# A hybrid decoder block on one core: modulation products put off, queries and keys normed in pairs, a row of numbers in PSUM, the last expert products ordered by tiles of tokens

## The chip, the cores and the metric

One core of one Trainium2 chip. The metric is the device time of the program in microseconds; three runs of the kernel before have a median of 2023.93 us (2022.27 to 2029.1). The engines are named as the profile names them: PE (matmuls), DVE (vector), ACT (scalar), POOL (GpSimd), SP (the queue that issues nearly all DMAs).

## The reference, cut to what matters

```
mod = silu(c) @ w_ada + b_ada                      # 6 x 1024 numbers: sh1, sc1, gt1, sh2, sc2, gt2
xn  = rms_norm(h) * (1 + sc1) + sh1                # 512 tokens x 1024 channels
qm, km, vm, zrw, gate_logits = split(xn @ w_in)
qm, km = rope(rms_norm(qm, q_norm_g)), rope(rms_norm(km, k_norm_g))     # per head of 64 channels
h   = h + gt1 * ((gated attention(qm, km, vm) + gated rwkv7(zrw)) @ w_out)
xn2 = rms_norm(h) * (1 + sc2) + sh2
s   = xn2 @ wq against 2 x 128 sub-keys, 8 heads; 16 best of each half; 16 best of their sums -> idx, gates
h   = h + gt2 * sum_k gelu(xn2 . u[idx_k]) * gates_k * v[idx_k]         # 16384 experts
```

The experts are computed densely for tokens 128 to 511 (all 128 groups of 128 experts, with a dense matrix of gates), and by gathered rows for tokens 0 to 127.

## The kernel before, in words

All of float32 is kept by splitting each operand into a high and a low part (`whi`, `wlo`; `vh`, `vl`; `ah`, `al`) and adding three products. Each engine runs its instructions in a fixed order, which a scheduler has written out at build time from the program's order, its priorities and the ordering hints that `follow(i, after)` gives; no hint costs a semaphore. The parts that matter here:

**Modulation.** `mod_col(ci, j)` multiplies a row block of `w_ada` (tile `wmod`, 512 KB, three buffers) by silu(c) and sums it on DVE, one instruction of 128x1024 (L176). Sixteen are needed at the start (sh1, sc1). The other 32, for gt1, gt2, sc2 and sh2, come from a generator, and `mods(1, i)` at the end of every product of a weight block (`w_cm`, L423; `w_tm`, twice, L456) takes one of them. `gate_rows` needs gt1 and gt2 after the twelfth gate product; sc2 and sh2 are needed in `out_norm`.

**Mixing.** `rwkv_in` computes the inputs of the recurrence (`decays`, `elementwise`, by DVE, POOL and ACT), with the products of L422 on PE. The recurrence over four chunks of 128 tokens (`inverses`, `tokens`, `state`, `group_norm`, tile `rwp`, L387) has a high priority, and other products fill PE between its steps: queries, keys and values (`qkv`, `w_tm`, L452), then attention and the sixteen gate products (`gates`, L422). In `qk_part`, for each half of the tokens, ACT copies the product to SBUF and squares it, DVE sums it per head and takes 1/sqrt by three Newton steps (12 instructions on 128x8, L574 and L161 to L166), POOL applies the gain and the rotation, DVE scales (`qn`, L589), and PE transposes the result (L594).

**Experts.** `queries` scores the sub-keys into PSUM (tile `atp`, three banks, L994) and finds the best 16 on DVE. `best_of` makes 50 candidates and picks their numbers: DVE compares (`eq`, L1026, 128x400, the row of numbers `iota` in SBUF), POOL (DVE for one tile of tokens) multiplies (L1027), DVE sums (L1029). `gates_dense` builds two one-hot matrices for each four tokens (`oh2`, L1221, on DVE, from a copy of `iota` that lies in PSUM; `ohg`, L1225 on DVE or L1230 and L1231 on ACT) and multiplies them on PE (`pg`, L1238), 96 times. Amid these, `dense_h` runs the products with U (L1178), its low parts on POOL (L1172). Then `dense_v` and `products` add the products with V into six PSUM banks `acc` (token tile t in banks 2t and 2t+1, L1305); the last two groups of experts are done together. At the end DVE scales each bank (L1335), DVE or POOL adds the residual (L1336), and SP stores it.

Of the kernel before, what the change touches and what calls it, by code (L numbers as in the profile page):

```python
# [10 lines left out]
F32 = mybir.dt.float32  # L11
# [5 lines left out]
ALU = mybir.AluOpType  # L17
# [12 lines left out]
NCAND = 50  # L30
# [33 lines left out]
def kernel(ctx: ExitStack, tc: tile.TileContext, A):  # L64
# [332 lines left out]

    nsplit = [0]

    def wload(src):  # L400
# [14 lines left out]
    def w_cm(w, x, k0, nk, n=512):  # L415

        hi, lo = w
        ps = mmtile()
        for k in range(nk):
            ks = slice((k0 + k) * 128, (k0 + k + 1) * 128)  # L420
            for n, (l, r) in enumerate(((hi, x[0]), (hi, x[1]), (lo, x[0]))):
                i = fill(PE.matmul(ps, l[:, ks], r(k), start=k == 0 and n == 0, stop=k == nk - 1 and n == 2), 512)  # L422
        mods(1, i)  # L423
        return ps
# [13 lines left out]
    def w_tm(src, x, halves=False):  # L438

        pss, ws = [mmtile() for _ in range(2)], {}  # L440
        todo = [(kh, tt) for kh in range(2) for tt in range(4)]
        if halves:
            todo.sort(key=lambda t: t[1] // 2)
        for kh, tt in todo:
# [10 lines left out]
            if tt == 3:  # L455
                mods(1, i)  # L456
        return pss
# [107 lines left out]

    def qk_part(ps, hf, qi, g):
        qf = ahalf("qn")
        qn = qf.rearrange("p (h j) -> p h j", h=8)
        ACT.copy(qf, ps)
        sq = ahalf("qsq").rearrange("p (h j) -> p h j", h=8)  # L570
        ACT.activation(sq, qn, AF.Square)
        ss = sm.tile([128, 8], F32, name="qss")
        DVE.tensor_reduce(ss, sq, axis=AX.X, op=ALU.add)
        DVE.tensor_scalar(ss, ss, 1.0 / 64, 1e-6, op0=ALU.mult, op1=ALU.add)  # L574
        y = sm.tile([128, 8], F32, name="qy")
        t = sm.tile([128, 8], F32, name="qt")
        newton(ss, y, t)
        POOL.tensor_tensor(qn, qn, qkg[:, qi:qi + 1].broadcast_to([128, 8, 64]), op=ALU.mult)
        r1, r2 = [at.tile([128, 2, 4, 16], F32, name=nm, bufs=1) for nm in ("r1", "r2")]
        x = qf.rearrange("p (i h j) -> p i h j", i=2, h=4)  # L580

        def table(n, a):
            return sincos[:, 2 * hf:2 * hf + 2, n:n + 1, a:a + 8 if n else 16].broadcast_to([128, 2, 4, 8 if n else 16])

        POOL.tensor_tensor(r1, x[:, :, :, 0:16], table(0, 0), op=ALU.mult)
        for a in (0, 8):
            POOL.tensor_tensor(r2[:, :, :, a:a + 8], x[:, :, :, 8 - a:16 - a], table(1, a), op=ALU.mult)
        POOL.tensor_tensor(x[:, :, :, 0:16], r1, r2, op=ALU.add)
        DVE.tensor_tensor(qn, qn, bc3(y, 64), op=ALU.mult)  # L589
        pT = attile()  # L590
        for c in range(2):
            for i in range(2):
                o = (2 * c + i) * 128
                PE.transpose(pT[:, o:o + 128], qf[:, i * 256 + c * 128:i * 256 + (c + 1) * 128], ident)  # L594
        dst = kvhalf("qkT")
        ACT.copy(dst, pT)
        for c in range(2):
            (qT, kT)[qi][hf, 2 * g + c] = v2(dst)[:, c]

    def qkv():  # L600
        for qi in (1, 0):
            for g in range(2):
                pss = w_tm(A["w_in_t"][2 * qi + g], X)
                for hf in range(2):
                    qk_part(pss[hf], hf, qi, g)
        for tt in range(4):
            vtok[tt] = kvhalf("vtok")
        for g in range(2):
            pss = w_tm(A["w_in_t"][4 + g], X)
            for tt in range(4):  # L610
                ACT.copy(vtok[tt][:, g * 256:(g + 1) * 256], pss[tt // 2][:, (tt % 2) * 256:(tt % 2 + 1) * 256])
# [272 lines left out]
    hd_ = [dr.tile([128, 4, 2, 256], F32, name=f"h_d{i}") for i in range(2)]  # L884
    vals, inds = {}, {}

# [115 lines left out]
    def best_of(tt, hh):  # L1002
# [20 lines left out]
        for j in range(8):  # L1023
            h_, k_ = j // 2, (j % 2) * 8
            eq = qg.tile([128, 8 * NCAND], F32, name="eq", bufs=3).rearrange("p (k n) -> p k n", k=8)
            DVE.tensor_tensor(eq, bc3(bf_[:, h_, k_:k_ + 8], NCAND), bcm(iota[:, 0:NCAND], 8), op=ALU.is_equal)  # L1026
            (DVE if tt in EQD else POOL).tensor_tensor(eq, eq, ci_[:, h_:h_ + 1].broadcast_to([128, 8, NCAND]), op=ALU.mult)  # L1027
            o = (8 * hh + j) * 8
            DVE.tensor_reduce(idf[tt][:, o:o + 8], eq, axis=AX.X, op=ALU.add)  # L1029
# [53 lines left out]
    qkv()  # L1083
    attend(0)
    gates(range(G0, G1))
    attend(1)
# [159 lines left out]

    queries(out_norm(mixer(o_rwkv)))

    iop.append(attile())
    ACT.copy(iop[0][:, 0:128], iota)  # L1250
# [47 lines left out]

    def products(es, parts):
        for t in range(3):  # L1300
            ts = slice(t * 128, (t + 1) * 128)
            for e, (ah, al, vh, vl) in zip(es, parts):
                for l, r in ((ah, vh), (ah, vl), (al, vh)):
                    for d in range(2):
                        i = PE.matmul(acc[2 * t + d], l[:, ts], r[:, d * 512:(d + 1) * 512],  # L1305
                                      start=e == 0 and l is ah and r is vh, stop=e == 127 and l is al)
        return i

# [104 lines left out]
```

## Time and profile before

| | |
|---|---|
| median of three runs | 2023.93 us |
| the profiled execution | 2025.54 us, span 2023.8 us, granted TensorE clock 0.979 |
| PE busy | 1915.9 us, 95% |
| DVE busy | 1510.3 us, 75% |
| ACT, POOL busy | 828.3 us (41%), 775.6 us (38%) |
| HBM traffic over the span | 222 GB/s |

By time from the span's start: to about 100 us the start and the first products; to about 560 us the recurrence, with queries, keys, values, attention and gates between its steps; to 712 us the output projection and its norm; to 800 us the queries of the experts; to 1215 us the dense gates and the first products with U; to 2014 us the products with V and the rest of those with U; then the stores. A busy time is the union of the instructions' durations; an instruction that is held in its engine counts as busy.

### The profile page before, as it was taken

What the parts mean: (1) busy time and instruction counts of PE and PEld (TensorE: products, weight loads), DVE (VectorE), ACT (ScalarE), POOL (GpSimd) and SP (SyncE); (2) the same over time, 40 slices, a digit from 0 to 9 for tenths busy, and PEclk for the clock granted to TensorE, in tenths of its full rate; (3) what the DMA queues carried; (4) which work ended last, traced back from release to release, by engine and by line L of the source; (5) the groups of instructions that cost most, each with busy time, mean ns of one, the idle gap of its engine ahead of it and who ended that gap; (6) DMA issues with size and microseconds to landing.
All of it is one profiled execution on the core that took longest, in us unless ns stands there. A gap on an engine that the chain in (4) does not pass through costs nothing.

```text
span 2023.8 us, 29453 instructions
## 1 busy us (share of the span) xinstructions
PE 1915.9 (95%) x10509; PEld 1669.0 (82%) x10509; DVE 1510.3 (75%) x3268; ACT 828.3 (41%) x1367; POOL 775.6 (38%) x631
## 2 busy tenths in 40 slices
PE   7987899999989899888999999999999999999997
PEld 5666777787868888877899998888899999999985
DVE  7798665546445578999977876888756788888885
ACT  5443233323313433356777763333333333333332
POOL 5555210010105322566656663222212444544551
PEclk9998899999989899999999999999999999999999
DMA  8664233321446423435568989999967999999893
GB/s 288 211 202 134 81 115 98 102 93 49 156 138 195 127 80 97 131 110 165 180 199 278 322 303 388 356 354 346 333 219 245 337 335 351 326 351 331 306 346 131
DMA packets 204326, 450.79 MB, mean 223 GB/s; under 512 B 16649, under 2 KB 105225, under 8 KB 204178
## 3 DMA queue, kind: packets, MB, share of 16 engines
q1 hardware_dynamic: 167024, 314.54, 46.1%
q0 software_dynamic: 36864, 134.23, 18.3%
q8 instruction: 83, 1.36, 0.3%
q14 instruction: 65, 0.53, 0.1%
q10 hardware_dynamic: 290, 0.13, 0.0%
HBM read 393.13 MB, written 55.71 MB: 222 GB/s over the span
## 4 chain that ended last, share of the span: by engine, by line
PE 69%; DVE 17%; DMA 4%; issue 2%; ACT 1%; POOL 0%; POOLq 0%; SPq 0%; DVEq 0%; ACTq 0%
PE acc L1305 23%; PE mm L1178 17%; PE mm L422 10%; PE rwp L387 8%; PE mm L452 4%; DMA vf<-in_peer_v 2%; PE pg L1238 2%; DVE ohg L1225 2%; DVE eq L1026 2%; DVE oh L1221 1%; DVE idf L1029 1%; DVE row L1143 1%; PE atp L868 1%; PE atp L842 1%; PE atp L994 1%
## 5 line engine op out<-in xcount | busy, mean ns | idle before, releaser
L1178 PE MATMUL mm<-x,whi 128*128 128x384 f32 x2048 | 542.2, 345 | 1.7 <-ACT ge L1183 1.7
L1178 PEld LDWEIGHTS mm<-x,whi 128*128 128x128 f32 x2048 | 372.7, 190 | 5.6 <-ACT ge L1183 2.0
L1178 PE MATMUL mm<-x,wlo 128*128 128x384 f32 x1024 | 350.8, 343 | 9.5 <-POOL wlo L1172 9.5
L1171 ACT CAST whi<-wf 128x1024 fp32r<-128x1024 f32 x128 | 134.7, 1052 | 290.8 <-PE mm L1178 223.7
L1305 PE MATMUL acc<-vl,ah 128*128 128x512 f32 x768 | 237.6, 390 | 2.7 <-DVE vl L1296 2.7
L1305 PE MATMUL acc<-vh,al 128*128 128x512 f32 x768 | 237.2, 390 | 0.0
L412 POOL TENSOR_TENSOR wlo<-wf,whi 128x1024 fp32r<-128x1024 f32 x33 | 80.9, 2450 | 399.2 <-ACT whi L409 309.9
L1305 PE MATMUL acc<-vh,ah 128*128 128x512 f32 x768 | 206.7, 390 | 3.3 <-ACT vh L1295 3.2
L1178 PEld LDWEIGHTS mm<-x,wlo 128*128 128x128 f32 x1024 | 194.6, 190 | 11.1 <-POOL wlo L1172 10.9
L1172 POOL TENSOR_TENSOR wlo<-wf,whi 128x1024 fp32r<-128x1024 f32 x66 | 163.5, 2479 | 102.4 <-ACT whi L1171 102.3
L1120 POOL DMA_INDIRECT row<-in_peer_u,gidx x96 | 113.2, 1179 | 233.2 <-DVE gh L1143 223.0
L1120 POOL DMA_INDIRECT row<-in_peer_v,gidx x86 | 124.1, 1443 | 154.1 <-DVE gacc L1150 142.5
L1296 DVE TENSOR_TENSOR vl<-vf,vh 128x1024 fp32r<-128x1024 f32 x128 | 157.5, 1231 | 22.5 <-ACT vh L1295 21.9
L1305 PEld LDWEIGHTS acc<-vh,ah 128*128 128x128 f32 x768 | 143.7, 188 | 34.5 <-ACT vh L1295 5.2
L1305 PEld LDWEIGHTS acc<-vl,ah 128*128 128x128 f32 x768 | 143.6, 188 | 31.0 <-DVE vl L1296 3.5
L1305 PEld LDWEIGHTS acc<-vh,al 128*128 128x128 f32 x768 | 144.1, 188 | 30.0
L1295 ACT CAST vh<-vf 128x1024 fp32r<-128x1024 f32 x128 | 134.7, 1054 | 17.2 <-DMA vf<-in_peer_v 17.2
L422 PE MATMUL mm<-X,whi 128*128 128x512 f32 x400 | 135.7, 411 | 3.3 <-ACT z L472 3.3
L1172 DVE TENSOR_TENSOR wlo<-wf,whi 128x1024 fp32r<-128x1024 f32 x62 | 75.9, 1224 | 84.1 <-ACT whi L1171 83.9
L1238 PE MATMUL pg<-ohg,oh 128*128 128x128 f32 x768 | 117.3, 287 | 22.0 <-ACT ohg L1231 15.2
L1143 DVE CUSTOM_DVE_ANT_0 row<-row,xtok 128x1024 f32<-128x1024 f32 x96 | 131.7, 1380 | 4.4 <-DMA row<-in_peer_u,gidx 4.4
L1238 PEld LDWEIGHTS pg<-ohg,oh 128*128 128x128 f32 x768 | 108.0, 192 | 31.6 <-ACT ohg L1231 19.0
(1195 smaller groups left out, 3807.5 us busy)
## 6 DMA issues: line engine op xcount, KB each, us to landing
wf<-in_peer_ut SPq DMA_DIRECT2D x128, 512.0 KB, 4.9
vf<-in_peer_v SPq DMA_DIRECT2D x128, 512.0 KB, 6.0
wmod<-in_w_ada SPq DMA_DIRECT2D x48, 512.0 KB, 4.3
G_d<-stg SPq DMA_DIRECT2D x12, 2048.0 KB, 9.4
wf<-in_w_in_c SPq DMA_DIRECT2D x30, 512.0 KB, 3.9
ge_d<-ge SPq DMA_DIRECT2D x50, 192.0 KB, 2.5
ger<-ge_d SPq DMA_DIRECT2D x50, 192.0 KB, 6.3
wf<-in_peer_wq SPq DMA_DIRECT2D x16, 512.0 KB, 3.5
```

Of the source, the lines that this page charges most:

```text
L387: i = f(*a, **k)
L422: i = fill(PE.matmul(ps, l[:, ks], r(k), start=k == 0 and n == 0, stop=k == nk - 1 and n == 2), 512)
L452: i = fill(PE.matmul(ps[:, c0:c0 + 256], l(4 * kh + k)[:, ts], r[:, cs], start=kh == 0 and tt % 2 == 0 and k == 0 and n == 0, stop=kh == 1 ...
L1120: i = POOL.indirect_dma_start(out=row, out_offset=None, in_=A[key], in_offset=bass.IndirectOffsetOnAxis(ap=gidx[:, s_:s_ + 1], axis=0))
L1143: DVE.tensor_tensor_reduce(out=row, in0=row, in1=xtok, op0=ALU.mult, op1=ALU.add, scale=1.0, scalar=0.0, accum_out=gh[:, s_:s_ + 1])
L1171: ACT.copy(uh, f)
L1172: (POOL if e < LAG else DVE).tensor_tensor(ul, f, uh.bitcast(F32), op=ALU.subtract)
L1178: i = PE.matmul(ps[:, 0:NTD], l[:, ks], r[:, k, 128:512], start=n == 0, stop=n == 23)
L1238: i = PE.matmul(pg[:, t * 128:(t + 1) * 128], oh2[:, t], ohg[:, t], start=True, stop=True)
L1295: ACT.copy(vh, f)
L1296: DVE.tensor_tensor(vl, f, vh.bitcast(F32), op=ALU.subtract)
L1305: i = PE.matmul(acc[2 * t + d], l[:, ts], r[:, d * 512:(d + 1) * 512], start=e == 0 and l is ah and r is vh, stop=e == 127 and l is al)
```

## The change

Four edits. `mods` takes its number from `nmod`: none in the products of the recurrence's inputs and of queries and keys, one in those of the values, two in every product after the first half of attention. `qk_parts` treats both halves of a product's tokens at once: one 1/sqrt on 128x16 in place of two on 128x8, and the transposes are issued later, hinted behind the third and fourth tile of the next product. A second copy of `iota` goes into a bank of `atp` before the queries, and `eq` reads it. In the last `products`, a hint keeps the matmuls of token tile t behind those of tile t-1.

```diff
+    nmod, marks = [0], []
@@ w_cm
-        mods(1, i)
+        mods(nmod[0], i)
@@ w_tm
+        marks.clear()
...
             if tt == 3:
-                mods(1, i)
+                mods(nmod[0], i)
+            marks.append(i)
@@
-    def qk_part(ps, hf, qi, g):
-        qf = ahalf("qn")
...
+    def qk_parts(pss, qi, g):
+
+        ss, y, t = [sm.tile([128, 2, 8], F32, name=n) for n in ("qss", "qy", "qt")]
+        qfs = []
+        for hf in range(2):
+            qf = ahalf("qn")
+            ACT.copy(qf, pss[hf])
+            sq = ahalf("qsq").rearrange("p (h j) -> p h j", h=8)
+            ACT.activation(sq, qf.rearrange("p (h j) -> p h j", h=8), AF.Square)
+            DVE.tensor_reduce(ss[:, hf], sq, axis=AX.X, op=ALU.add)
+            qfs.append(qf)
         DVE.tensor_scalar(ss, ss, 1.0 / 64, 1e-6, op0=ALU.mult, op1=ALU.add)
         newton(ss, y, t)
...
+        def channels_first(after):
+            for hf, qf in enumerate(qfs):
+                pT = attile()
+                for c in range(2):
+                    for i in range(2):
+                        o = (2 * c + i) * 128
+                        m = PE.transpose(pT[:, o:o + 128], qf[:, i * 256 + c * 128:i * 256 + (c + 1) * 128], ident)
+                        follow(m, after[hf])
...
+        return channels_first
@@ qkv
                 pss = w_tm(A["w_in_t"][2 * qi + g], X)
-                for hf in range(2):
-                    qk_part(pss[hf], hf, qi, g)
+                if later:
+                    later.pop()(marks[2:4])
+                later.append(qk_parts(pss, qi, g))
...
+            nmod[0] = 1
             pss = w_tm(A["w_in_t"][4 + g], X)
+            if later:
+                later.pop()(marks[2:4])
@@ best_of
-            DVE.tensor_tensor(eq, bc3(bf_[:, h_, k_:k_ + 8], NCAND), bcm(iota[:, 0:NCAND], 8), op=ALU.is_equal)
+            DVE.tensor_tensor(eq, bc3(bf_[:, h_, k_:k_ + 8], NCAND), bcm(ioe[0][:, 0:NCAND], 8), op=ALU.is_equal)
@@
     attend(0)
+    nmod[0] = 2
@@
-    queries(out_norm(mixer(o_rwkv)))
-
+    first_q = out_norm(mixer(o_rwkv))
+
+    ioe.append(attile())
+    ACT.copy(ioe[0][:, 0:128], iota)
+    queries(first_q)
@@ products
+            ts, last = slice(t * 128, (t + 1) * 128), i
...
+                        if len(es) > 1:
+                            follow(i, last)
```

On DVE, while the recurrence's first chunk begins (`C`, `Dk`: its first inverse; `qss`, `qy`, `qt`: the 1/sqrt of the keys; `wmod`: a modulation product). Before:

```order
L166 SCALAR_TENSOR_TENSOR qy<-qt,qy 128x8
L164 TENSOR_TENSOR qt<-qy 128x8
L645 TENSOR_TENSOR Dk<-C,dl_558 128x512
L166 SCALAR_TENSOR_TENSOR qy<-qt,qy 128x8
L164 TENSOR_TENSOR qt<-qy 128x8
L165 SCALAR_TENSOR_TENSOR qt<-qt,qss 128x8
L176 ISA wmod,modc<-wmod,scr 128x1024
L176 ISA modc 128x1
L164 TENSOR_TENSOR qt<-qy 128x8
L165 SCALAR_TENSOR_TENSOR qt<-qt,qss 128x8
L166 SCALAR_TENSOR_TENSOR qy<-qt,qy 128x8
L645 TENSOR_TENSOR Dk<-C,dl_558 128x512
```

and now:

```order
L658 TENSOR_REDUCE C<-cm__1279 128x64
L166 SCALAR_TENSOR_TENSOR qy<-qt,qy 128x16
L663 TENSOR_TENSOR Dk<-C,dl_558 128x512
L595 TENSOR_TENSOR qn<-qn,qy 128x512 x2
L663 TENSOR_TENSOR Dk<-C,dl_558 128x512
L413 TENSOR_TENSOR wlo<-wf,whi 128x1024
```

The modulation product is gone from between the two `Dk`, and so are the second chains of the 1/sqrt; both scalings `qn` of a pair stand together.

On PE, the transposes of the second pair of keys (`atp<-ident,qn`) and the first matmuls that wait for the first inverse (`rwp<-ident,XT`). Before, half of the pair stood directly ahead of them:

```order
L452 MATMUL mm<-wlo,X 128x256
L594 MATMUL atp<-ident,qn 128x128 x4
L387 MATMUL rwp<-ident,XT 128x128 x4
L387 MATMUL rwp<-RR,Bq 128x128 x4
L452 MATMUL mm<-whi,X 128x256 x2
```

and now the whole pair stands amid the next product:

```order
L454 MATMUL mm<-whi,X 128x256
L603 MATMUL atp<-ident,qn 128x128 x8
L454 MATMUL mm<-whi,X 128x256
L454 MATMUL mm<-wlo,X 128x256
L454 MATMUL mm<-whi,X 128x256 x2
L454 MATMUL mm<-wlo,X 128x256
L387 MATMUL rwp<-ident,XT 128x128 x4
L387 MATMUL rwp<-RR,Bq 128x128 x4
```

Eight transposes, where there were four with four more further on, now stand five matmuls ahead of `rwp<-ident,XT`.

On PE at the end of the program, the start of the last group's matmuls (the six banks have consecutive numbers, two for each tile of tokens). Before, they ran over all three tiles by part:

```order
L1305 MATMUL acc_11816<-vh,ah 128x512
L1305 MATMUL acc_11817<-vh,ah 128x512
L1305 MATMUL acc_11818<-vh,ah 128x512
L1305 MATMUL acc_11819<-vh,ah 128x512
L1305 MATMUL acc_11820<-vh,ah 128x512
L1305 MATMUL acc_11821<-vh,ah 128x512
L1305 MATMUL acc_11816<-vl,ah 128x512
```

and now, for the last two groups together, one tile after the other (here the first tile, both groups):

```order
L1329 MATMUL acc_11758<-vh,ah 128x512
L1329 MATMUL acc_11759<-vh,ah 128x512
L1329 MATMUL acc_11758<-vl,ah 128x512
L1329 MATMUL acc_11759<-vl,ah 128x512
L1329 MATMUL acc_11758<-vh,al 128x512
L1329 MATMUL acc_11759<-vh,al 128x512
L1329 MATMUL acc_11758<-vh,ah 128x512
L1329 MATMUL acc_11759<-vh,ah 128x512
L1329 MATMUL acc_11758<-vl,ah 128x512
```

The first tile's two banks are complete 24 matmuls ahead of the last one, where they were complete 8 ahead.

## Rows read from the trace of the kernel before

**Rows 1.** [...]

```profile
60.00:100.00 40.00, 39.48 (x146) 25.21 (x146) 33.45 (x41) 15.88 (x24) 23.26 (x21) 1.00 0.63 204
...
160.00:180.00 20.00, 12.57 (x54) 9.50 (x52) 19.83 (x56) 5.24 (x9) 12.46 (x15) 0.66 0.64 210
...
200.00:220.00 20.00, 11.70 (x63) 10.61 (x62) 14.93 (x51) 4.66 (x8) 6.89 (x11) 0.67 0.25 79
220.00:240.00 20.00, 20.00 (x169) 19.64 (x169) 10.55 (x18) 2.85 (x4) 5.40 (x5) 0.99 0.16 53
...
300.00:350.00 50.00, 50.00 (x314) 38.42 (x313) 27.17 (x66) 14.96 (x44) 4.71 (x2) 1.00 0.35 108
...
850.00:900.00 50.00, 42.76 (x238) 40.87 (x236) 50.00 (x150) 24.50 (x41) 33.95 (x38) 0.95 0.37 125
900.00:950.00 50.00, 41.74 (x247) 39.07 (x246) 50.00 (x154) 30.78 (x50) 30.28 (x30) 0.97 0.54 163
...
1200.00:1280.00 80.00, 78.16 (x382) 68.62 (x381) 50.13 (x72) 28.70 (x39) 31.75 (x21) 1.00 1.00 370
...
1440.00:1930.00 490.00, 490.00 (x2478) 448.22 (x2477) 382.73 (x440) 174.11 (x234) 198.63 (x154) 1.00 0.87 310
```

**Rows 2.** Waits of PE from 96 to 215 us: who waited for whom, us in total, times, longest. The first and the last of eight rows, which sum to 25.1 us.

```profile
PE atp L594 <- DVE qn L589: 8.3, 1, 8.3
PE rwp L387 <- DVE Dk L645: 4.5, 1, 4.5
...
PE mm L452 <- ACT qn L569: 1.5, 1, 1.5
```

**Rows 3.** The chain that ended last, pieces with start and length in us: the first and the last of the three modulation products on it, and the place where the wait of Rows 2 ends.

```profile
140.18 1.13 DVE wmod L176
...
200.98 1.14 DVE wmod L176
...
211.36 1.11 PE atp L594 x4
212.48 2.86 PE rwp L387 x12
```

**Rows 4.** Groups of DVE instructions from 100 to 215 us by line: output and inputs, shape, count, busy us, mean ns of one, idle time before them.

```profile
L176 DVE CUSTOM_DVE_ANT_0 wmod<-wmod,scr 128x1024 f32<-128x1024 f32 x9 | 11.9, 1325 | 0.0
...
L165 DVE SCALAR_TENSOR_TENSOR qt<-qt,qss 128x8 f32<-128x8 f32 x18 | 4.1, 226 | 0.1
...
L164 DVE TENSOR_TENSOR qt<-qy 128x8 f32<-128x8 f32 x18 | 3.2, 180 | 0.1
```

**Rows 5.** Waits of PE from 215 to 560 us (the first two rows; all four sum to 5.2 us), and the longest waits of DVE from 300 to 550 us.

```profile
PE rwp L387 <- DVE Dk L645: 3.0, 2, 1.6
PE atp L842 <- ACT P L849: 0.9, 1, 0.9
...
DVE atp L845 <- PE atp L842: 35.2, 19, 4.3
...
DVE P L686 <- PE rwp L387: 10.7, 7, 4.2
```

**Rows 6.** Waits of the SP queue from 90 to 600 us: the longest total.

```profile
SPq L175 <- DVE modc L176: 51.3, 13, 19.1
```

**Rows 7.** Instructions by line, with ns of one (least/median/most): the comparison `eq`, the one-hot comparison that reads PSUM, and a product of two SBUF tiles; then, for `eq`, the group with its mean from 800 to 1200 us and who waited for it.

```profile
L1026 DVE TENSOR_TENSOR eq<-wa,iota x64: 522/566/2701, 822.1 to 1027.6; 128x400 f32<-128x400 f32 x64
...
L1221 DVE TENSOR_TENSOR oh<-sT,atp x96: 664/678/690, 874.6 to 1197.7; 128x512 f32<-128x512 f32 x96
...
L589 DVE TENSOR_TENSOR qn<-qn,qy x8: 683/692/693, 177.2 to 249.7; 128x512 f32<-128x512 f32 x8
...
L1026 DVE TENSOR_TENSOR eq<-wa,iota 128x400 f32<-128x400 f32 x64 | 54.6, 880 | 0.0
...
  POOL eq L1027: 34.7, 26
```

**Rows 8.** Waits of PE from 800 to 1215 us, all but one row of 1.7 us.

```profile
PE pg L1238 <- ACT ohg L1231: 15.2, 12, 2.8
PE mm L1178 <- POOL wlo L1172: 9.5, 3, 5.5
PE pg L1238 <- DVE ohg L1225: 6.6, 7, 2.8
```

**Rows 9.** Score matmuls of one head and the copies out of their PSUM bank, in order of time: start us, length, engine, line.

```profile
741.65 0.59 ACT L996 COPY sc__6736<-atp 128x512 f32<-128x512 f32 x1
...
747.45 0.60 PE L994 MATMUL atp<-keys,pq__6795 128*128 128x128 f32 x4
```

**Rows 10.** The end of the program in order of time: start us, length, engine, line; x is the number of instructions merged.

```profile
2005.44 1.52 PE L1305 MATMUL acc<-vh,ah 128*128 128x512 f32 x6
...
2006.73 1.23 DVE L1296 TENSOR_TENSOR vl<-vf,vh 128x1024 fp32r<-128x1024 f32 x1 [0.43 <-ACT vh L1295]
...
2011.76 1.29 DVE L1335 TENSOR_TENSOR o<-acc,gt 128x512 f32<-128x512 f32 x2 [3.81 <-PE acc L1305]
...
2013.15 0.61 PE L1305 MATMUL acc<-vh,al 128*128 128x512 f32 x2
...
2018.02 1.26 POOL L1336 TENSOR_TENSOR o<-o,hh 128x512 f32<-128x512 f32 x1 [1.83 <-DVE o L1335]
```

More of the change, by code (lines that the diff above doesn't have):

```diff
@@ L564 @@
     qT, kT, vtok = {}, {}, {}
-    def qk_part(ps, hf, qi, g):
-        qf = ahalf("qn")
[L568 to L573, printed above, removed]
+    def qk_parts(pss, qi, g):
[8 more added lines that the diff above has]
+            qfs.append(qf)
@@ L574, in qk_part @@
         DVE.tensor_scalar(ss, ss, 1.0 / 64, 1e-6, op0=ALU.mult, op1=ALU.add)
-        y = sm.tile([128, 8], F32, name="qy")
-        t = sm.tile([128, 8], F32, name="qt")
         newton(ss, y, t)
[L578 to L598, printed above, removed]
+        for hf, qf in enumerate(qfs):
+            qn = qf.rearrange("p (h j) -> p h j", h=8)
+            POOL.tensor_tensor(qn, qn, qkg[:, qi:qi + 1].broadcast_to([128, 8, 64]), op=ALU.mult)
+            r1, r2 = [at.tile([128, 2, 4, 16], F32, name=nm, bufs=1) for nm in ("r1", "r2")]
+            x = qf.rearrange("p (i h j) -> p i h j", i=2, h=4)
+            def table(n, a):
+                return sincos[:, 2 * hf:2 * hf + 2, n:n + 1, a:a + 8 if n else 16].broadcast_to([128, 2, 4, 8 if n else 16])
+            POOL.tensor_tensor(r1, x[:, :, :, 0:16], table(0, 0), op=ALU.mult)
+            for a in (0, 8):
+                POOL.tensor_tensor(r2[:, :, :, a:a + 8], x[:, :, :, 8 - a:16 - a], table(1, a), op=ALU.mult)
+            POOL.tensor_tensor(x[:, :, :, 0:16], r1, r2, op=ALU.add)
+            DVE.tensor_tensor(qn, qn, bc3(y[:, hf], 64), op=ALU.mult)
@@ new lines, in channels_first @@
+        def channels_first(after):
+            for hf, qf in enumerate(qfs):
+                pT = attile()
[4 more added lines that the diff above has]
+                        follow(m, after[hf])
+                dst = kvhalf("qkT")
+                ACT.copy(dst, pT)
+                for c in range(2):
+                    (qT, kT)[qi][hf, 2 * g + c] = v2(dst)[:, c]
@@ L600, in qkv @@
+        return channels_first
     def qkv():
+        later = []
         for qi in (1, 0):
@@ L884 @@
     hd_ = [dr.tile([128, 4, 2, 256], F32, name=f"h_d{i}") for i in range(2)]
-    vals, inds = {}, {}
+    vals, inds, ioe = {}, {}, []
     def top16(src, v, ix):
@@ L1299, in products @@
     def products(es, parts):
+        i = None
         for t in range(3):
-            ts = slice(t * 128, (t + 1) * 128)
+            ts, last = slice(t * 128, (t + 1) * 128), i
             for e, (ah, al, vh, vl) in zip(es, parts):
```

## The prediction

> **What bounds the kernel now.** I read the page first: PE is busy 95% of the span, so a change gains only where PE waits or runs at its lower clock, and it gains elsewhere only by shortening the end. So the next view is the table of windows, read for stretches in which PE is not full. [rows 1] has them. From 60 to 100 us PE is full. [...] From 220 us on PE is full again, and DVE about half. From 850 to 950 us DVE is busy every microsecond and PE 41 to 43 of 50. From 1440 to 1930 us PE is full.
>
> The third view is who ends PE's waits. From 96 to 215 us they sum to 25.1 us, nearly all ended by DVE [rows 2]; from 800 to 1215 us to 33.0 us, on one-hots from ACT and DVE and on low parts from POOL [rows 8]. The last two name ACT and POOL, but POOL itself waits 34.7 us for DVE's `eq` [rows 7], and its low parts stand in its queue behind those multiplications. So two stretches hang on DVE, and the rest on PE. The end, from the last matmul to the last store, hangs on the order of the banks [rows 10].
>
> **First stretch, 100 to 215 us.** The change takes nine modulation products of 1.325 us off DVE there, 11.9 us [rows 4], and half of the small 1/sqrt instructions: three pairs, 72 instructions become 36. One costs 0.18 to 0.23 us as it stands [rows 4], so the 36 that go are worth at most 8 us; where they alternate with others their durations overlap, and I take 5. Sum 17 us on an engine that is nearly always busy in the stretch. Six more modulation products go before 100 us; they gain nothing, as PE is full until then. I count 16 us for the stretch. The transposes that move amid the next product take away the 8.3 us wait for `qn`, but alone they would give about 1 us: directly behind them, at 212.48, PE runs the transposes of the inverse `XT` [rows 3], which come out of DVE's same queue, so that chain is late next, and only a shorter DVE queue brings it forward. Bounds: at least the three products that lie on the chain, 3 x 1.13 = 3.4 us [rows 3]; at most all of PE's waits, 25.1, and what the lower clock costs. That is, from the windows at 0.66 and 0.67, 2 x 20 x 0.33 = 13 us at the lower level, half of it lost if PE were busy throughout, 7 us; so 32. From 220 us on PE is full, its waits to 560 us sum to 5.2 us [rows 5], and the order on PE hardly changes, so what is gained here stays gained.
>
> **Where the products go.** Four are done with the values and 28 in pairs behind the gate products, from about 250 to 500 us, some 15 more there than before, about 18 us of DVE work. The cover is DVE's idle time: it is busy 27 of 50 us [rows 1], and it waits for PE (10.7 us in 7 waits at one step of the recurrence, 35.2 us in 19 at the scores [rows 5], so 1.5 to 1.9 us each). A pair holds DVE for 2 x 1.22 = 2.4 us, more than such a wait by up to 0.9 us; behind it stand the recurrence's next step, on which PE waits, and the scores. PE has some 2 us of other products behind each step, and for single products it waited 5.2 us in all. I take a loss of 3 us; bounds 0 and 14 pairs x 0.9 = 13. The loads of `wmod` move with them into a stretch where DMA is busy 0.35 in place of 0.64 [rows 1].
>
> **`eq` reads PSUM.** 64 of them take 0.880 us on average, with a median of 0.566 and a most of 2.701 [rows 7]: the excess is time in which a POOL instruction held them. The nearest row for the new form is `oh` (L1221), one input in SBUF, one in PSUM, amid the same POOL work: 96 of them, never above 0.690 us [rows 7]. So I expect every `eq` at about 0.566, and 64 x (0.880 - 0.566) = 20 us less on DVE between 822 and 1028 us. At the price of `oh`, which has 512 elements where `eq` has 400, it would be 64 x 0.20 = 13 us. DVE is full there, and three quarters of 20 us, 15, should come to PE: its waits, 33 us, are larger, but not all hang on DVE, and POOL's next holds fall on other DVE instructions. Bounds: 0, if ACT and POOL turn out to set the pace themselves, and 33. From 1200 to 1280 us DMA is full [rows 1], but PE still runs 78 of 80, so a shift of all that stands before passes through.
>
> [...]
>
> The bank for `iota` leaves two for the scores. I cost it at nothing: the second copy out of a bank ends at 742.2 and the next score matmuls start at 747.45 [rows 9], and that gap of 5 us covers it. Without the cover each of eight heads would wait for one copy of 0.59 us, 5 us in all.
>
> **The end.** Now the last matmul ends at 2013.76 us and POOL's last addition at 2019.28, 5.5 us later, since all six scalings come within 2 us of PE's end [rows 10]. With tiles in order, two tiles are scaled, added and stored while PE still runs (24 and 12 matmuls ahead, of 0.227 us each: six in 1.36 us), and behind the last matmul stand two scalings (1.29) and one addition on POOL (1.26): 2.6 us, so 2.9 less. Against that, the last group's low part `vl` ends at 2007.96, and with tiles in order PE comes to it after eight matmuls from 2005.44, at 2007.26: a wait of 0.7 us that was covered before by sixteen other matmuls. Net 2.2 us; bounds 1 and 3.
>
> **Sum.** 16 + 15 + 2.2 - 3 = 30.2 us. Against the profiled execution, 2025.5 us (span 2023.8 and 1.7 around it), that is 1995.3; that execution is 1.6 us above the median of the runs, 2023.9, so the forecast for the median is 1994 us. About 0.3%, 6 us, is what a measurement of this kernel can tell from no change.
>
> **Rivals.**
> 1. *The gates' stretch doesn't follow DVE.* For it: ACT ends most of the waits there, 15.2 us [rows 8]. Against it: DVE full from 850 to 950. Then only the first stretch and the end count: 2009 us.
> 2. *The first stretch follows POOL and ACT rather than DVE.* POOL is busy 12.46 of 20 us from 160 to 180 and holds DVE instructions. Then 4 us come in place of 16: 2006 us.
> 3. *Nearly all of PE's waits go in both stretches*, and its clock stays up: 25 + 25 + 2 - 3 = 49, so 1975 us.
> 4. *Pairs land on PE in full.* If each of 14 pairs cost PE all of 2.44 us, that is 34 us where I count 3, and the time would be 2025 us. Against it: DVE's idle half.
> 5. *Slower: SP's queue.* The loads of `wmod` already stand in SP's queue for DVE, 51.3 us in all [rows 6], and the load of the next gate's weights stands behind them. With two in a row, paced by the gate product before, each of 16 gates could get its weights late. It decides from 33 / 16 = 2.1 us a gate on; at 3 us each it costs 48 us: 2039 us. Against it: three weight buffers, and no such wait of PE now.
>
> **How the numbers follow.** The forecast 0.52, rivals 1 to 5 0.17, 0.13, 0.08, 0.05, 0.05. Faster by over 0.3% are the forecast and rivals 1 to 3, 0.90, less a little for both losses of rivals 1 and 2 together with a larger loss in the pairs: 0.88. Within 0.3%: rival 4 and that case, 0.07. Slower: rival 5, 0.05. The range reaches to rival 3 and past rivals 1 and 2: 1975 to 2012 us, with rivals 4 and 5 left out. The forecast's own range, by half of the distance to the bounds, is 1984 to 2004.
>
> **What the profile after would show.** From 160 to 220 us PE busy over 17 of 20 us and its clock near 1; the wait of `atp` for `qn` gone; 220 us's full stretch begins some 16 us earlier. Between 250 and 500 us PE's waits below 10 us. `eq` with a most below 0.7 us, POOL's wait for it below 15 us, PE's waits in the gates' stretch about half. The last POOL addition 3 us behind the last matmul. Wrong would be: DVE still full in the gates' stretch with `eq` short (other instructions held in its place), or the full stretch at the old time.

## The result, and the profile after

The changed kernel took 2005.18 us (median of 5 runs, 2005.01 to 2009.61) beside 2022.27 us for the kernel before on the same chip: a ratio of 0.9918, with a 95% interval of 0.9906 to 0.9931, so 17 us less. Run again beside the later experiments it had 0.9947 (0.9928 to 0.9965), 11 us less. The forecast of 1994 us lies outside both; the range of 1975 to 2012 holds the first. Of the forecast 30 us about half came, by the second measurement a third.

The profiled execution has 2009.6 us, with a span of 2007.8. These are its windows, as in [rows 1]: start, end and length in us; busy time of PE, of its weight loads, of DVE, ACT and POOL, each with the number of its instructions; then the granted TensorE clock (in this trace and in that of before it is 1.00 or 0.50 at any time, and a window shows the mean), the busy share of the DMA engines, and GB/s.

```profile
60.00:100.00 40.00, 40.00 (x149) 25.95 (x149) 25.21 (x33) 17.58 (x26) 20.77 (x24) 1.00 0.40 135
160.00:180.00 20.00, 11.85 (x61) 9.35 (x59) 16.29 (x32) 5.41 (x10) 8.75 (x13) 0.74 0.44 131
200.00:220.00 20.00, 18.09 (x107) 16.90 (x108) 11.76 (x25) 1.40 (x3) 4.53 (x5) 0.74 0.09 27
220.00:240.00 20.00, 20.00 (x185) 19.47 (x184) 11.71 (x26) 6.51 (x11) 8.48 (x11) 1.00 0.25 79
850.00:900.00 50.00, 42.82 (x240) 41.21 (x239) 49.98 (x180) 26.82 (x44) 34.79 (x41) 0.90 0.33 110
900.00:950.00 50.00, 43.03 (x260) 40.89 (x259) 50.00 (x144) 34.60 (x58) 31.54 (x38) 0.97 0.59 182
```

From 160 to 180 us DVE is no longer full (16.29 where [rows 1] have 19.83), and yet PE is busy no longer than before. From 850 to 950 us DVE is as full as before, which the prediction had named as a sign of being wrong; what that means here is said in the section on the prediction.

The waits of PE from 96 to 215 us, which answer to [rows 2]:

```profile
PE rwp L387 <- DVE Dk L663: 8.1, 1, 8.1
PE rwp L387 <- DVE XT L686: 3.3, 1, 3.3
PE mm L423 <- ACT z L475: 2.3, 1, 2.3
```

The wait of `atp` for `qn`, 8.3 us, is gone; one of 8.1 us for `Dk` stands in its place. Pieces of the chain that ended last, around that wait (start, length):

```profile
151.12 0.67 DVE kk L520
...
161.32 2.27 DVE qt L164
...
168.74 0.65 DVE Dk L663
169.44 2.94 PE rwp L387 x6
```

From 151.1 to 169.4 us this chain lies on DVE alone. About half of it, 9.4 us, is work of the 1/sqrt (`qss`, `qy`, `qt`), two of its small instructions drawn out to 1.2 and 2.3 us.

PE's waits from 800 to 1215 us, as in [rows 8], all but one row of 0.5 us:

```profile
PE pg L1257 <- ACT ohg L1250: 15.0, 12, 2.8
PE mm L1197 <- POOL wlo L1191: 4.8, 3, 2.7
PE pg L1224 <- DVE ii L1220: 3.6, 1, 3.6
PE mm L1197 <- ACT ge L1202: 1.4, 1, 1.4
PE pg L1257 <- DVE ohg L1244: 1.1, 2, 0.6
```

The comparison `eq` is as was expected from [rows 7], none over 0.572 us; POOL's wait for it fell less. The line of `eq` with its durations (ns, least/median/most), and who waited for it:

```profile
L1044 DVE TENSOR_TENSOR eq<-wa,atp x64: 514/558/572, 818.8 to 1011.8; 128x400 f32<-128x400 f32 x64
...
  POOL eq L1045: 26.8, 19
```

**Where the time went.** PE runs the same 10,509 matmuls in every kernel of this study. So the start of its n-th matmul in the trace before, less that in another trace, is the lead of the other kernel there. The table gives it in us, at places where both orders have the same instruction:

| n (us before) | changed | again | iota | mods | qk | tail | no mods | singles | low | ci | singles+ci | singles+pool |
|---|---|---|---|---|---|---|---|---|---|---|---|---|
| 1000 (239) | 8.9 | 11.0 | -0.5 | 11.1 | 2.2 | 0.0 | 3.4 | 12.1 | 10.2 | 9.4 | 13.3 | 11.0 |
| 3000 (553) | 2.6 | 4.6 | -0.5 | 4.4 | 1.8 | -0.1 | 3.0 | 11.5 | 3.9 | 3.0 | 11.1 | 10.4 |
| 4400 (808) | 3.3 | 0.5 | 0.3 | 4.8 | 2.6 | 1.1 | 3.8 | 12.0 | 4.5 | 2.3 | 7.2 | 7.1 |
| 5600 (1044) | 15.2 | 13.4 | 12.5 | 5.3 | 6.5 | 1.3 | 15.7 | 24.0 | 16.4 | 20.6 | 25.5 | 14.8 |
| 7200 (1332) | 15.6 | 11.0 | 13.4 | 7.2 | 6.0 | 0.5 | 13.4 | 23.0 | 13.5 | 19.8 | 23.9 | 14.6 |
| last (2013) | 13.3 | 8.7 | 13.4 | 7.2 | 4.6 | -0.4 | 11.2 | 20.7 | 11.2 | 17.5 | 21.6 | 12.4 |

(The columns are the kernels of the next section, one execution each.) The changed kernel gains 9 to 11 us up to 240 us, gives 6.4 of them back by 553 us, gains 12 us between 808 and 1044 us, and loses 2.0 from there to its last matmul. The scatter of one execution can be seen where a kernel has no edit: at 239 us `iota` and `tail` have -0.5 and 0.0, but `qk` moves by 3.8 us in the gates' stretch, and the changed kernel run again lost 4.0 us between 553 and 808 us where it gained 0.8 the first time. So single stages are told to about 2 us, worse in those two places. The loss between 553 and 808 us may be more than scatter: the three executions that have it (3.3 to 4.0 us: the changed kernel again, `singles_ci`, `singles_pool`) are the three that were run on another chip than the other experiments, and the rest lie between 0.7 lost and 1.2 gained there. The kernel before was not slower on that chip (a median of 2022.77 us beside 2024.15 and 2025.09); no run tells more.

The parts of the first profile add up: 8.9 - 6.4 + 0.8 + 11.9 + 0.4 up to 1332 us, then 2.3 lost to the last matmul and 2.7 gained behind it, 16 us in all, which is the difference of the two spans.

### The profile page after: what moved, and what is told of

Same layout as the page of the kernel before. It is cut to its first block, busy times and chain, and to the rows that moved or that the text cites. A ratio compares the mean times of both kernels' runs of the same rounds, so it can differ in the third digit from the quotient of the medians.

```text
span 2007.8 us, 29400 instructions
## 1 busy us (share of the span) xinstructions
PE 1913.9 (95%) x10509; PEld 1670.2 (83%) x10509; DVE 1490.1 (74%) x3220; ACT 827.5 (41%) x1368; POOL 764.2 (38%) x631
## 4 chain that ended last, share of the span: by engine, by line
PE 69%; DVE 17%; DMA 3%; ACT 2%; issue 1%; POOL 1%; POOLq 0%; SPq 0%; DVEq 0%; ACTq 0%
PE acc L1329 25%; PE mm L1197 17%; PE mm L423 9%; PE rwp L387 8%; PE mm L454 4%; DVE ohg L1244 2%; PE pg L1257 2%; DVE oh L1240 2%; DVE eq L1044 1%; DVE idf L1047 1%; DVE row L1162 1%; PE atp L860 1%; PE atp L886 1%; DMA vf<-in_peer_v 1%; DVE eq L1045 1%
## 5 line engine op out<-in xcount | busy, mean ns | idle before, releaser
L1257 PEld LDWEIGHTS pg<-ohg,oh 128*128 128x128 f32 x768 | 108.0, 195 | 23.1 <-ACT ohg L1250 18.8
```

The source lines that it names most:

```text
L1257: i = PE.matmul(pg[:, t * 128:(t + 1) * 128], oh2[:, t], ohg[:, t], start=True, stop=True)
```

## Experiments: each edit alone

**iota_alone**: the kernel before, with

```
+    ioe.append(attile())
+    ACT.copy(ioe[0][:, 0:128], iota)
-            DVE.tensor_tensor(eq, ..., bcm(iota[:, 0:NCAND], 8), op=ALU.is_equal)
+            DVE.tensor_tensor(eq, ..., bcm(ioe[0][:, 0:NCAND], 8), op=ALU.is_equal)
```

> The kernel before with the PSUM copy of the row of numbers alone. Theory (the gates' stretch follows DVE; what the 64 comparisons give up, 20.7 us, comes to PE less the holds that fall on other DVE instructions, 9 us): about 12 us faster than before (10 to 14), the comparisons at 0.56 us with none above 0.7, and DVE's other instructions of the stretch some 9 us longer in sum than before. Rival (part of the 12 us of the whole change came from PE reaching the stretch earlier by the other edits): under 6 us faster.

Measured: 2011.61 us, ratio 0.9936 (0.9913 to 0.9958), 13 us less; lead from 0.3 to 12.5 us in the gates' stretch. As the theory said. What "hold" means can be measured: for each DVE instruction, its length above the shortest of the same form, summed where that is over 0.3 us (the form is the line, the tiles and the shapes). From 800 to 1050 us this excess was 41.2 us on 33 instructions before, 20.1 of them on the comparison. With the comparison reading PSUM it is 28.8 us on 24, none on the comparison: of the 20 us some 7.7 fell on other instructions. DVE's saving is 12.4 us, and PE gained 12.2: here PE follows DVE one to one. One of the new victims, in the changed kernel (ns, least/median/most; 128 x 128):

```profile
L1219 DVE TENSOR_SCALAR ii<-ii x3: 227/981/2341, 859.6 to 1017.8; 128x128 int32<-128x128 int32 x3
```

By the trace, 22.8 of the 28.8 us lie on instructions that run beside POOL's low parts `wlo` (2.4 us each) and end within 0.5 us of them; the other 6.0 end in the same way with POOL's multiplications `eq` (1.0 us each). Why an instruction of DVE is held beside these, no run shows. With one input in PSUM, 64 of 64 comparisons are free of it, none above 0.572 us in the changed kernel.

**mods_alone**: the kernel before, with `mods(1, i)` made `mods(nmod[0], i)`, which is 0 up to the queries, 1 with the values, 2 from the gates on.

> The kernel before with the modulation products put off, and nothing else. Theory (they carry most of the 9 us lead that the changed kernel has at 240 us, and all of the 6 us that it loses again up to 560 us): lead of 6 to 8 us at 240 us, 0 to 3 us left at 560 us, and 0 to 3 us faster in the end. Rival (the lead comes from the queries and keys by pairs, the products bring only the loss): no lead at 240 us, 3 to 6 us slower in the end.

Measured: 2019.10 us, 0.9982 (0.9963 to 1.0000). The lead is more than expected at 239 us, 11.1, and 4.4 are left at 553: the products that are put off do carry the first lead, and their new places bring the loss behind it.

**qk_alone**: the kernel before, with `qk_parts` in place of `qk_part` and the transposes put behind `marks[2:4]`.

> The kernel before with queries and keys by pairs amid the next products, and nothing else. Theory (DVE's queue from 100 to 215 us sets the pace, and 36 small instructions of 0.2 us go from it while the products stay): 2 to 4 us faster at 240 us, and kept to the end, as no pairs of products follow: 2 to 4 us faster. Rival (this edit carries the lead): 6 to 9 us faster at 240 us and in the end.

Measured: 2025.34 us, 1.0006 (0.9990 to 1.0022). The lead of 2.2 us at 239 us is there, but it is not to be seen in the time, and the 2 to 4 us at the end that the theory had are not met. The 3.8 us that its execution gained in the gates' stretch are chance, as nothing is changed there.

**tail_alone**: the kernel before, with the last `products` in the order of the tiles (`follow(i, last)`).

> The kernel before with the last products over V by tiles of tokens, and nothing else. Theory (the last work behind the last matmul shrinks by 2.7 us, the last low part is late by 0.5 to 0.9 us): 1.8 to 2.2 us faster, at the edge of what can be told. Rival (the time behind the last matmul is set by the last store's own length): no change, within 0.5 us.

Measured: 2023.85 us, 1.0005 (0.9988 to 1.0022): unclear. The trace shows both halves. From the end of the last matmul (2014.1) to the end of the span (2021.5) are 7.4 us, where it was 10.0 before; and the matmuls of the last group wait 0.5 us for `vl` and run slower around that wait (two right behind it take 0.73 us, 0.62 elsewhere), so that PE ends 0.9 us later. The end in the changed kernel, as in [rows 10] (start, length; in brackets the idle time before it):

```profile
1992.55 1.22 DVE L1318 TENSOR_TENSOR vl<-vf,vh 128x1024 fp32r<-128x1024 f32 x1 [0.43 <-ACT vh L1317]
...
1993.83 0.73 PE L1329 MATMUL acc<-vl,ah 128*128 128x512 f32 x2 [0.52 <-DVE vl L1318]
...
1999.87 0.61 PE L1329 MATMUL acc<-vh,al 128*128 128x512 f32 x2
2000.35 1.29 DVE L1361 TENSOR_TENSOR o<-acc,gt 128x512 f32<-128x512 f32 x2 [0.89 <-issue]
...
2001.72 1.64 POOL L1362 TENSOR_TENSOR o<-o,hh 128x512 f32<-128x512 f32 x1 [1.12 <-DVE o L1361]
```

POOL's last addition ends 2.9 us behind PE, where it was 5.5.

## Experiments: what gives the lead back, and what limits the first stretch

**no_mods**: the changed kernel with `nmod` at 1 throughout.

> The changed kernel with the modulation products where they stood before, one behind each product; the other three edits stay. Theory (the put-off products give the lead of 9 us at 240 us and take 5 to 6 us of it back by 560 us, so they are worth 2 to 4 us in the end): 2009 us, 2 to 4 us slower than the changed kernel, lead over before of 2 to 3 us at 240 us and the same at 560 us. Rival (with queries and keys by pairs the products no longer matter): the same time as the changed kernel within 1 us.

Measured: 2011.16 us, 0.9934 (0.9916 to 0.9953). By the traces it has 3.4 us at 239 us and keeps 3.0 at 553, as the theory said; at 553 us that is as much as the changed kernel has (2.6 and 4.6). So in the changed kernel what the products gain in the first stretch is about what they lose behind it. At the last matmul `no_mods` leads by 11.2 us, the changed kernel by 13.3 and 8.7: this edit is worth nothing that can be told.

**singles**: the changed kernel, with

```
     attend(0)
-    nmod[0] = 2
     gates(range(G0, G1))
     attend(1)
     gates(range(G1, 12))
+    mods(1)
     gate_rows(2, 5)
+    nmod[0] = 2
     gates(range(12, 16))
+    nmod[0] = 1
     proj(0, ...)
```

> The changed kernel with one modulation product behind each gate product up to the twelfth, two behind the last four, and one behind each product of the first projection, in place of pairs behind every gate product. Theory (two in a row hold DVE 2.4 us, and that is what gives 6 us of the lead back between 250 and 560 us): lead over before still 6 to 8 us at 560 us, 3 to 5 us faster than the changed kernel. Rival (the lead is given back whatever the products do, since PE comes earlier to steps of the recurrence that other work sets): the lead at 560 us stays at 2 to 4 us, same time as the changed kernel.

Measured: 2005.70 us, 0.9907 (0.9882 to 0.9932), beside 2011.16 for `no_mods` on the same chip. Of 12.1 us at 239 us it keeps 11.5 at 553, where the changed kernel keeps 2.6 of 8.9. The other two kernels with single products, below, keep 11.1 of 13.3 and 10.4 of 11.0; all five executions with pairs (the changed kernel twice, `mods_alone`, `low_on_dve`, `ci_psum`) give 6.3 to 6.7 us back. So the pairs bring the loss. The times alone don't tell `singles` from the changed kernel (0.9907 beside 0.9918 and 0.9947).

What the loss consists of is seen at one place. The changed kernel, PE around 526 us (start, length; idle time before), then windows of it:

```profile
523.61 0.40 PE L423 MATMUL mm<-X,whi 128*128 128x512 f32 x1
526.07 1.26 PE L387 MATMUL rwp<-hy,sel8t 8*128 8x128 f32 x8 [2.06 <-DVE hy L166]
527.26 2.07 PE L387 MATMUL rwp<-XX,At 128*128 128x128 f32 x8
```

```profile
527.00:530.40 3.40, 3.40 (x13) 2.90 (x13) 1.38 (x2) 0.00 (x0) 2.19 (x2) 0.50 0.49 145
240.00:260.00 20.00, 18.20 (x121) 15.37 (x118) 9.63 (x22) 6.91 (x17) 2.35 (x1) 0.91 0.18 53
395.00:415.00 20.00, 19.07 (x110) 14.98 (x110) 13.90 (x33) 4.52 (x13) 4.49 (x3) 0.91 0.41 124
520.00:540.00 20.00, 17.85 (x102) 15.06 (x101) 8.75 (x21) 4.32 (x7) 4.93 (x3) 0.91 0.37 119
```

The last three windows in `singles`, and the same eight matmuls there:

```profile
240.00:260.00 20.00, 17.29 (x110) 13.17 (x109) 12.11 (x30) 8.67 (x24) 2.35 (x1) 1.00 0.18 55
395.00:415.00 20.00, 20.00 (x123) 15.77 (x121) 12.59 (x34) 6.85 (x17) 2.73 (x3) 1.00 0.39 122
520.00:540.00 20.00, 20.00 (x124) 17.34 (x122) 11.53 (x20) 5.85 (x10) 2.37 (x1) 1.00 0.79 248
```

```profile
525.36 1.05 PE L387 MATMUL rwp<-XX,At 128*128 128x128 f32 x8
```

Eight matmuls of 1.05 us in all took 2.07 behind the wait: the granted clock was 0.50 there. A granted clock of 0.91 over 20 us is 1.8 us lost, and there are three such places, at 247, 404 and 527 us, which neither `singles` nor the kernel before has (1.00 in all three windows of both): 5.4 us. PE's waits themselves grew by little, from 5.2 us in [rows 5] to 7.0 here:

```profile
PE rwp L387 <- DVE hy L166: 3.0, 2, 2.1
PE rwp L387 <- DVE Dk L663: 2.8, 3, 1.8
PE atp L860 <- ACT P L867: 0.9, 1, 0.9
PE mm L378 <- DVE dg L377: 0.3, 2, 0.2
```

1.8 and 5.4 make 7.2, against 6.4 given back. (From the 1000th to the 3000th matmul PE's idle time is 7.3 us where it was 5.5, and its busy time 312.6 where it was 308.0.) `mods_alone` and `low_on_dve` fall at 246, 403 and 526 us too, the changed kernel run again and `ci_psum` at about 400 and 524 (the dip at 247 is not in those two).

So all five executions with pairs wait for `hy` twice, 0.9 and 2.1 us, and each time the lower clock follows. A wait alone doesn't bring it: `singles` waits 1.8 us at 242 and 1.9 at 356 us, the kernel before 1.6 and 1.4, and their clock stays at 1.00. Nor can the dip at 247 us be put down to the pairs, as the wait ahead of it, 1.8 us for `Dk`, is in `singles` too.

The experiment's theory on how pairs do it, that two in a row hold DVE, is not what these two places show. DVE around 518 us in the changed kernel:

```profile
514.13 0.08 DVE L176 DVE_READ_ACCUMULATOR2_ANT modc<- 128x1 f32 x1
518.31 0.28 DVE L840 TENSOR_SCALAR hv<-rwp 8x128 f32<-8x128 f32 x1 [4.10 <-PE rwp L387]
```

The pair is done 4.1 us before `hv`, the start of the chain to `hy`, and DVE sits idle for PE in between; at 394 us it is the same with 1.6 us. What differs as well is PE's order, which the scheduler wrote anew: from the 1000th to the 3000th matmul another instruction stands at 1,323 of 2,000 places than before, in `mods_alone` at 1,284, in `singles` at 329 and in `no_mods` at 67. That this order leaves too little work behind `hy` is likely; no run shows it.

**low_on_dve**: the changed kernel, with

```
-        eng = DVE if nsplit[0] % 2 else POOL
+        eng = DVE if nsplit[0] % 2 or 8 <= nsplit[0] <= 16 else POOL
```

> The changed kernel with the five low parts that POOL makes between 100 and 215 us made by DVE, 1.22 us each in place of 2.6. Theory (in that stretch instructions of DVE are drawn out by POOL's low parts, 10.5 us by the excess of each over the shortest of its form, so DVE ends its queue 10.5 - 6.1 = 4 us sooner): lead at 240 us 3 to 4 us more than with the changed kernel, 2 to 4 us faster. Rival (DVE's waits for the chain in front of it hide the drawn out instructions; its own added work does not hide): lead 0 to 4 us less.

Measured: 2011.82 us, 0.9935 (0.9919 to 0.9951); lead at 239 us 10.2, amid the 8.9 to 13.3 of the changed kernel and of those that equal it up to there. The holds went, from 22.9 to 10.1 us by the excess (96 to 215 us), and at 239 us nothing of it is left. DVE and PE from 96 to 215 us, before, in the changed kernel and in this one:

```profile
96.00:215.00 119.00, 93.88 (x509) 72.43 (x507) 106.66 (x232) 44.12 (x70) 58.95 (x60) 0.89 0.52 166
```

```profile
96.00:215.00 119.00, 100.80 (x558) 80.41 (x557) 93.92 (x173) 43.83 (x70) 57.74 (x60) 0.90 0.37 119
```

```profile
96.00:215.00 119.00, 100.84 (x568) 80.45 (x567) 90.84 (x179) 44.44 (x71) 44.96 (x55) 0.90 0.36 119
```

DVE is idle 12 us before, 25 in the changed kernel, 28 here, and PE is busy as long in the last two. What DVE waits for in the changed kernel, the first four rows:

```profile
DVE G L758 <- PE rwp L387: 4.7, 3, 3.8
DVE ee L500 <- ACT e L497: 3.5, 2, 1.9
DVE wlo L413 <- ACT whi L410: 3.3, 1, 3.3
DVE kk L520 <- POOL KK L518: 3.2, 3, 1.1
```

They are spread over PE, ACT and POOL. A window of fixed bounds can't tell what became of a saving, as later work moves into it; so the same work, from the 325th to the 1000th matmul: DVE is busy 114.7 us before, 99.4 in the changed kernel and 95.7 in `low_on_dve`, and the work takes 139.1, 131.5 and 130.2 us. (The five other executions of the changed kernel's code there take 127 to 130.)

Yet PE did get some of this saving on its way. From the 425th to the 800th matmul it gains 1.9 us on the changed kernel, where the five other executions of that code stay within 0.03 us of it, and its wait for `Dk` is 5.6 us in place of 8.1. Then it loses it all at `XT` (waits of PE, then the chain ahead of it):

```profile
PE rwp L387 <- DVE Dk L663: 5.6, 1, 5.6
PE rwp L387 <- DVE XT L686: 4.7, 1, 4.7
```

```profile
195.85 1.23 DVE wlo L413
...
199.10 0.74 DVE XT L686
```

Two low parts, of 1.23 us each, stand amid DVE's steps to `XT` here, and none in the changed kernel, where that wait is 3.3 us. So the theory falls in its size, and the run doesn't show that DVE's queue has ceased to matter: what counts is what stands ahead of `Dk` and `XT`, not the sum of DVE's work.

## Experiments: the gates' stretch, and a faster version

**ci_psum**: the changed kernel, with

```
+        if tt in EQD:
+            pc = ioe[0][:, 64 + 200 * hh:264 + 200 * hh].rearrange("p (j n) -> p j n", j=4)
+            ACT.copy(pc, ci_)
+            ci_ = pc
...
-    ACT.copy(ioe[0][:, 0:128], iota)
+    ACT.copy(ioe[0][:, 0:64], iota[:, 0:64])
```

> The changed kernel with the numbers of the candidates of the one tile of tokens that DVE multiplies itself read from PSUM (16 multiplications of 128x400, mean 0.989 us in the changed kernel, median 0.565), by two copies of ACT. Theory (a hold that finds its instruction gone falls on the next one that reads SBUF alone, as four tenths of those of the comparisons did): the 16 at 0.57 us each, 6.9 us less on DVE, but the excess of all DVE instructions in the gates' stretch falls only from 28 to about 24 us, and the time by 2 to 4 us. Rival (holds are a property of the instruction): the excess falls by the full 6.9 us, to 21, and the time by 5 to 7 us.

Measured: 2005.21 us, 0.9904 (0.9884 to 0.9924), beside 2011.82 and 2011.16 for `low_on_dve` and `no_mods` on the same chip; lead from 2.3 to 20.6 us in the stretch, 18.3 where the changed kernel gains 12 to 13. The 16 products:

```profile
L1049 DVE TENSOR_TENSOR eq<-eq,atp x16: 544/562/566, 821.1 to 850.6; 128x400 f32<-128x400 f32 x16
```

The excess of all DVE instructions fell from 28.8 to 18.8 us, by 10, where the theory had 4 and the rival 7: both fall in size. PE gained about 6 of the 10, and DVE waited 3.4 us more over the same matmuls. Where the holds of the comparisons fell to a third on others, here others were freed as well (`ii`, 8.8 us in the changed kernel, has 1.5). Which instructions are held beside a low part was not the same in the two executions, and the sum over them was not foreseen.

**after_again**: the changed kernel as it is.

> The changed kernel once more, on the chip of the runs beside it. Every theory: ratio to before 0.990 to 0.993. Its lead at 240 us tells the scatter of the first stretch: if the 9 us of the first profile were its true size, 8 to 10 again; if the lower clock's few microseconds fall differently in each execution, anything from 8 to 12 us, with the give back of 6 to 7 us by 560 us the same.

Measured: 2012.38 us (2009.34 to 2015.08, 8 runs), 0.9947 (0.9928 to 0.9965): a smaller gain than the first time, at the edge of the two intervals. Lead 11.0 at 239 us and 4.6 at 553, so 6.5 given back again.

**singles_ci**: both edits together, `singles` and `ci_psum`.

> The changed kernel with both edits: modulation products one by one, and the candidates' numbers of the one tile of tokens in PSUM. Theory (the two act in stretches apart, 5 to 6 us between 250 and 560 us and 5 us between 800 and 1050 us, and nothing behind takes them back): 8 to 11 us faster than the changed kernel, about 1995 us, ratio to before 0.985 to 0.987. Rival (the second stretch gives the same end whatever came before it): 5 us faster, ratio 0.988 to 0.990.

Measured: 2001.49 us, 0.9903 (0.9877 to 0.9929) beside 0.9947 for the changed kernel on the same chip: 11 us faster than it by the medians. It has the lowest median of all, but its ratio to before is that of `ci_psum` (0.9904) and `singles` (0.9907), so that the two edits add is shown by the traces and by that one comparison. The traces agree with the sum of the two (11.1 us at 553, a further 18.3 between 808 and 1044), less 3.9 lost between, at the place named above. The ratio to before lies by the rival's number rather than the theory's, as before itself ran from 2012 to 2029 us in this set; between the two kernels the theory's 8 to 11 us are met.

**singles_pool**: `singles` with `EQD = ()`.

> The changed kernel with modulation products one by one, and the 16 multiplications that DVE makes for one tile of tokens (15.8 us on DVE with their holds) made by POOL like the other 48, 0.97 us each. Theory (DVE's queue sets the pace from 800 to 1030 us; POOL is busy two thirds there): DVE gets 12 to 16 us less to do and PE 6 to 12 us of it, so 6 to 12 us faster than with the products one by one alone. Rival (at that place DVE waits for POOL in each of 16 rounds, as the reduction needs the product at once): DVE idle by as much as it gained, no change within 2 us.

Measured: 2010.01 us, 0.9942 (0.9921 to 0.9962). The lead in the stretch is 7.7 us where `singles` has 12.0: worse, by neither number. The rival's reason isn't it either: the reduction waited for the product 0.6 us in all.

```profile
L1047 DVE TENSOR_REDUCE idf<-eq x64: 539/554/570, 821.0 to 1001.5; 128x8 f32<-128x400 f32 x64
its engine sat idle before it (us, times) until:
  POOL eq L1045: 0.6, 1
```

DVE was rid of 15.8 us of work, 6.9 of them holds, and yet its excess by holds is 29.9 us where `singles` has 28.8: 8 us of holds fell on other instructions. Over the same matmuls (808 to 1044 us before) DVE is busy only 3.9 us less, POOL 14.3 us more, and DVE is idle 14.2 us in place of 6.1, at the one-hots `oh` above all, for PE and ACT. So what DVE gave up came back as holds and waits; why PE then lost 4 us is left open.

## Why the prediction was right and where it was wrong

**The sign, the stretches and the range: right,** the range at its slow end: the second measurement, 2012.38 us, lies just outside it. The three places gain as named: up to 240 us, from 808 to 1044 us, the end; and time is lost between 250 and 553 us.

**First stretch: 16 us forecast, 9 to 13 came** (six executions of the same code up to there). The count of DVE's work was right: no product stands there any more (11.9 us), and the 1/sqrt instructions of the stretch (those with `qt` and `qy`, 14.9 us before) take 9.8, the 5 us that were taken. The step that failed is "I count 16 us for the stretch", that PE gets what DVE saves. Over the same matmuls DVE's busy time fell by 15.3 us and the time by 7.7 (8 to 12 in the six): the rest became idle time of DVE, which now waits for PE, ACT and POOL. That is rival 2 in part, at half its price or less. But the two longest waits of PE that are left end with DVE's `Dk` (8.1 us) and `XT` (3.3), ahead of which DVE runs without a pause. `XT` was named as late next; `Dk` was overlooked. From 160 to 180 us PE is busy 11.85 us, not over 17, and its clock of 0.66 came up to 0.74, not to near 1.

The upper bound there has a slip that decided nothing: with 0.50 as the lower level, which the trace of before has from 166 to 179 and from 207 to 220 us, a mean of 0.66 over 20 us is some 13 us at that level in each of the two windows, 27 in all, of which 13 are lost; the prediction has half of both.

**The products in pairs: 3 us forecast, 6.4 came.** The step "I take a loss of 3 us" fails in two things. It leaves out the clock, which fell behind waits of 0.9 to 2.1 us in a stretch that was full, to 0.91 over 20 us at three places, 5.4 us in all. And it lets a pair hold DVE, while the two waits for `hy` that came don't stand behind a pair. That "the order on PE hardly changes" was wrong too (1,323 of 2,000 places), and with it that "what is gained here stays gained". PE's waits grew by 1.8 us, near the 3 that were taken, by luck as far as the runs show. The upper bound of 13 held the loss. Rival 5 did not come; SP's waits for `wmod` grew from 51.3 us [rows 6] to 64.5, and no wait of PE for these weights shows.

**`eq` in PSUM: 15 us forecast, 12 came.** All 64 are free, some 20 us, as worked out. Both halves of what followed were off, and they nearly cancel, so that the size is partly luck: holds of 7.7 us fell on others, and nearly all of what is left, not three quarters, reached PE. The sign of being wrong, DVE still full with `eq` short and other instructions held in its place, did show, but it takes back only those 7.7 us: DVE is full since it sets the pace, and it is through with this work 12 us sooner. POOL's wait for `eq` fell from 34.7 us to 26.8, not below 15, and PE's listed waits from 33.0 to 26.4, not to half. The input in PSUM cost nothing that shows: the median went from 0.566 to 0.558 us, as 512 elements with one input in PSUM had taken 0.678 us where both in SBUF took 0.692 [rows 7].

**The end: 2.2 us forecast, 1.8 by the traces** (2.7 gained behind PE, 0.9 lost before it). The times can't tell it.

**Not foreseen:** a loss of 1.4 us between 1332 and 1989 us (below), and that a measurement of this kernel scatters by more than the 6 us I gave it.

## What to carry to other kernels

Before crediting PE with what leaves a busy engine, see what stands ahead of each of PE's waits: here one stretch followed DVE one to one (12.2 us of 12.4), and the other passed on half to four fifths (8 to 12 us of 15.3) and turned the rest into waits on three engines. Work that was put off into a stretch where PE is full was better put off singly: 11.5 us of the lead were left behind it, with pairs 2.6; there, in the first profile, waits of 0.9 and 2.1 us were each followed by a clock of 0.91 over 20 us, 1.8 us lost each time, more than the waits in sum. And of the holds that the comparisons lost by reading PSUM, 20.1 us, 7.7 fell on their neighbours, so take the excess of all instructions as the measure, not that of the one.

## What the runs showed of the hardware that was not expected

In a full stretch, waits of PE of 0.9 and 2.1 us were followed by the lower clock in all five executions that have them: in the changed kernel a granted clock of 0.91 over 20 us, 1.8 us lost (rows above), and in its second execution 0.91 and 0.83. Waits of 1.4 to 1.9 us elsewhere were not, in `singles` and in the kernel before; and one of 1.6 us at 543 us, the same in both, was followed by it in `singles_ci` and not in `singles`. What decides isn't shown.

What is taken off one instruction of DVE that is held beside POOL is not what DVE gains: with 20.1 us of holds gone from the comparisons, the excess of all its instructions fell by 12.4 us, and with 6.9 more gone from the multiplications it fell by 10.0.

From 1332 to 1989 us PE does the same in every kernel, in the same order, and full but for three waits of about 1 us that every kernel has. Yet all nine kernels with the queries and keys by pairs take 1.4 us more for it (1.37 to 1.43), and the three others of the study (`iota_alone`, `mods_alone`, `tail_alone`) 0.0. It is spread over hundreds of the 3,200 matmuls, never more than 11 ns at one. What it comes from isn't known.
